# A second copy of the high parts in PSUM for the subtraction of the split products

## The chip, the cores and the metric

The kernel runs on one core of a Trainium2 chip. The metric is the device time of one execution in microseconds, taken as the median over runs. TensorE (PE) multiplies, VectorE (DVE), ScalarE (ACT) and GpSimd (POOL) do elementwise work, and SyncE (SP) issues the DMAs. SBUF is the on-chip memory, PSUM the memory of eight banks into which PE writes its products.

## The reference, cut to what is computed

One layer of a hybrid trunk on a sequence of 1024 rows of 1024 channels, float32. Four token mixers are fed by one projection, merged by gates and projected; an FFN with a short convolution follows.

```python
h = rms_norm(x, tm_pre_g) * (1.0 + sc_t) + sh_t
p = split_columns(h @ w_in)
y_ml, y_gla, y_conf, y_sc = ...        # mLSTM, gated linear attention, Conformer and short convolution
gates = jax.nn.sigmoid(p["gate"] + merge_gate_b).reshape(B, S, 4, D)
y = (gates[:, :, 0] * y_ml + ... + gates[:, :, 3] * y_sc) @ w_o
x = x + g_t * rms_norm(y, tm_post_g)
h = rms_norm(x, cm_pre_g) * (1.0 + sc_c) + sh_c
a, v = jnp.split(causal_dwconv(h @ w_up, dw_w), 2, axis=-1)     # width 3, hidden 2816
x = x + g_c * rms_norm((jax.nn.silu(a) * v) @ w_down, cm_post_g)
```

## The kernel before

Everything is held transposed, channels on the 128 partitions, and the rows of the sequence in two halves of 512. A matrix product in float32 is made of products of a reduced-width type (fp32r): each operand is split into a high part (the operand rounded, a cast on ACT) and a low part (the operand minus its high part, a subtraction on DVE or POOL), and a product of one 128-row slab is three matmuls, hi by hi, hi by lo and lo by hi. The function split (line 255) makes the two parts; wsplit, wslab, h_split, split2, tsplit and wpair call it. The high and low parts of weights lie in the tags wh and wl (four buffers each) or fh and fl (six), those of the moving operand in B11, B21, B22 and T1 to T4. The large products are computed by a 2x2 block scheme with seven products in place of eight, so that sums and differences of blocks are formed on POOL and DVE beforehand, and then split.

The stages follow one another: a first part with the conditioning and the norm (0 to 125 us), the projections and mixers P and G, the gated merge E, the output projection with the first products of the FFN O, the up-projection F (22 rounds, from the 17th on all seven products, before that five), and the down-projection W (four accumulators of 11 steps for each product; in the code p1, a second one with the same accumulators, p5, p3, p6, p7, p4). In a round of F the products with the weights s2a, s2b, s2c and s2d stand beside the evictions of the round and the width-3 convolution of the round before: ACT's first tap (an activation from SBUF into a PSUM bank), two multiply-adds on DVE on that bank, and a Silu on ACT. The last product of a round, "22" (finish, line 1536 and after), is issued in the next round, and its eviction feeds the third and fourth tap. In W the step's two operands are loaded, summed on DVE (p5, p7) or POOL (p3, p6, p4, and r2 in p5), and split; then 12 matmuls follow.

A scheduler places the instructions on the engines. Only what ordered names is kept in the program's order: POOL in P and G, PE in W. Each engine works its queue in order. All loads are on SP's queue. PSUM is one pool with eight banks, each 128x512 floats, and mps (line 180) takes the next one; ps1 and ps2 in W are four accumulators each, so the eight banks of W are held from its start.

Each operation goes through one wrapper, so that its line reads L157, and the tiles' names tell it apart (numbers of buffers left out: b is a PSUM bank, c a four-buffer work tile of the tag c4).

Of the kernel before, what the change touches and what calls it, by code (L numbers as in the profile page):

```python
# [9 lines left out]
F32 = mybir.dt.float32  # L10
F32R = mybir.dt.float32r
U32 = mybir.dt.uint32
AF = mybir.ActivationFunctionType
ALU = mybir.AluOpType
# [130 lines left out]
def trunk_layer(ctx: ExitStack, tc: tile.TileContext, I, out, dump=None, stop=None):  # L145
# [15 lines left out]
    V, A, G, T = (InOrder(e, n) for e, n in ((nc.vector, "V"), (nc.scalar, "A"), (nc.gpsimd, "G"), (nc.tensor, "T")))  # L161
# [7 lines left out]
    def new(tag, shape, dt=F32, bufs=1, pool=sb):  # L169
        uid[0] += 1  # L170
        return pool.tile(shape, dt, tag=tag, name=f"{tag}_{uid[0]}", bufs=bufs)

    c4 = lambda shape=(P, S): new("c4", list(shape), bufs=4)
    def pool(name):
        st = ctx.enter_context(ExitStack())
        return st, st.enter_context(tc.tile_pool(name=name, bufs=1))
# [3 lines left out]
    mps = lambda: new("b", [P, HS], bufs=8, pool=pb_)  # L180
# [26 lines left out]
    def pc(nm, n=0, w=1):  # L207
        o = PCOL[nm][0] + n
        return par[:, o:o + w]
# [41 lines left out]
        nc.sync.dma_start(dst, d.partition_broadcast(P))  # L251

    vl, hl, pe_last = [None], [None], [None]

    def split(src, hi, lo, eng=None, bias=None):
        if bias is None:
            hl[0] = A.copy(hi, src).ins
            vl[0] = (eng or V).tensor_tensor(lo, src, hi.bitcast(F32), ALU.subtract).ins
        else:
            A.activation(hi, src, AF.Identity, bias=bias)  # L260
            last[0] = V.scalar_tensor_tensor(lo, src, bias, hi.bitcast(F32), ALU.add, ALU.subtract).ins

    def wsplit(src, eng=None):
        hi = new("wh", [P, HS], F32R, bufs=4)
        lo = new("wl", [P, HS], F32R, bufs=4)
        split(src, hi, lo, eng)
        return hi, lo
# [20 lines left out]
    def h_split(nm, kk, src, eng=None, bias=None):  # L288
        split(src, *BM[nm][kk], eng, bias)
# [115 lines left out]
    def scaled(k):  # L405
        sc = mod[:, 8 + k:9 + k]
        x1 = xt[:, k, HH[1]]
        hi0 = A.activation(X(k, 0)[0], xt[:, k, HH[0]], AF.Copy, scale=sc).ins
        if k == 0:
            with tc.issue_after(hi0):  # L410
                square(0)
        A.activation(x1, x1, AF.Copy, scale=sc)
        split(x1, *X(k, 1), G)
        if k == 0:
            for i in (1, 2):
                with tc.issue_after(hi0):
                    std_slab(i, 0)
            more(0)
# [110 lines left out]
    def operands():  # L529
        t2 = [t[:, i, :] for t in (c4((P, 2, HS)), c4((P, 2, HS))) for i in range(2)]  # L530
        for kk in range(4):
            normed(kk, 1, G)
            with tc.issue_after(los[4 + kk]):
                normed(kk + 4, 1)
            G.tensor_tensor(xh(kk, 0), xh(kk, 1), xh(kk, 0), ALU.subtract)
            G.tensor_tensor(t2[kk], xh(kk + 4, 1), xh(kk, 0), ALU.subtract)
            yield
        new_bm("T2")
        for kk in range(4):
            h_split("T2", kk, t2[kk], bias=bias(kk + 4))  # L540
            if kk % 2:
                yield
        new_bm("T1")
        for kk in range(4):
            h_split("T1", kk, xh(kk, 0), G)
            G.tensor_tensor(xh(kk, 1), xh(kk + 4, 1), xh(kk, 1), ALU.subtract)
            V.tensor_tensor(xh(kk + 4, 0), t2[kk], xh(kk + 4, 0), ALU.subtract)
            if kk % 2:
                yield
        new_bm("T3")  # L550
        for kk in range(4):
            h_split("T3", kk, xh(kk, 1), bias=shd[:, kk:kk + 1])
            if kk % 2:
                yield
        new_bm("T4")
        for kk in range(4):
            h_split("T4", kk, xh(kk + 4, 0), G)
        new_bm("22")
        for kk in range(4):
            h_split("22", kk, xh(kk + 4, 1), bias=bias(kk + 4))  # L560
        yield
# [90 lines left out]
    mgp.close()  # L652

    ordered[0] = IN_ORDER["P"]

    mxp, mx = pool("mxp")
    s1 = lambda shape=(P, MIX): new("s1", list(shape), bufs=5, pool=mx)
# [698 lines left out]
    exp_.close()  # L1356

    ordered[0] = IN_ORDER["O"]

    fzp, fz = pool("fz")  # L1360
    dx1 = new("dx1", [P, KT, S], pool=dr)
# [145 lines left out]
    ffp, ff = pool("ff")  # L1507

    ordered[0] = IN_ORDER["F"]
    def conv_pair(n, ca, cv):  # L1510

        t = c4()
        for src, w in ((cv, NF + n), (ca, n)):
            for h in range(2):
                o = h * HS
                p_ = mps()
                A.activation(p_, src[:, o + 2:o + 2 + HS], AF.Copy, scale=pc("fdw", 3 * w + 2))
                V.scalar_tensor_tensor(p_, src[:, o + 1:o + 1 + HS], pc("fdw", 3 * w + 1), p_, ALU.mult, ALU.add)
                V.scalar_tensor_tensor(t[:, HH[h]] if w > n else p_, src[:, o:o + HS], pc("fdw", 3 * w), p_,
                                       ALU.mult, ALU.add)  # L1520
                if w == n:
                    A.activation(p_, p_, AF.Silu)
                    V.tensor_tensor(t[:, HH[h]], p_, t[:, HH[h]], ALU.mult)
        nc.sync.dma_start(dg[n], t)
# [8 lines left out]
    for n in range(NF):  # L1533
# [37 lines left out]
        if prev:  # L1571
            conv_pair(*prev[0:3])
# [10 lines left out]
        V.scalar_tensor_tensor(cv[:, lo_], pd, -1.0, u2, ALU.mult, ALU.add)  # L1583
    finish(prev)
    conv_pair(*prev[0:3])
    if stop == "F":
        return
# [34 lines left out]
    def keep():  # L1622
        ts = [new("acc", [P, 2, HS], bufs=8, pool=dn) for _ in range(2)]
        vs = [t[:, i, :] for t in ts for i in range(2)]
        pair_of.update((id(v), ts[i // 2]) for i, v in enumerate(vs))
        return vs
# [5 lines left out]
    def split2(t, a, eng):  # L1632
        th = [new("B21", [P, HS], F32R, bufs=8) for _ in range(2)]
        split(t, *th)
        return th, wsplit(a, eng)

    def mm(ps, kk, d, th, wh, new_):
        for i, (w_, t_) in enumerate(((wh[0], th[0]), (wh[0], th[1]), (wh[1], th[0]))):
            lm[0] = T.matmul(ps[d], w_[:, d * P:(d + 1) * P], t_, start=(new_ and kk == 0 and i == 0),
                             stop=(kk >= NK - 1 - LE and i == 2), skip_group_check=not new_ or kk > NK - 1 - LE).ins  # L1640

    def run(ps, operands, new_, eng=None, each=None):
        for kk in range(NK):
            th, wh = split2(*operands(kk), eng)
            for d in range(4):
                mm(ps, kk, d, th, wh, new_)
            if each:
                each(kk)

    g11, g12, g22, r1, r2 = ([None] * NK for _ in range(5))  # L1650
    ps1, ps2 = [mps() for _ in range(4)], [mps() for _ in range(4)]

    def p1(kk):
        g11[kk], r1[kk] = load(slot(), g(kk, 0, 0)), load(slot(), w(kk, 0, 0))
# [11 lines left out]
    def p5(kk):  # L1666
# [5 lines left out]
        G.tensor_tensor(r2[kk], a22, r1[kk], ALU.subtract)  # L1672
        return g11[kk], a22

    run(ps2, p5, True)
    c22 = keep()
    for d in range(4):
# [29 lines left out]
    def p6(kk):  # L1707
        G.tensor_tensor(g11[kk], g22[kk], g11[kk], ALU.subtract)
        return g11[kk], r2[kk]

    run(ps1, p6, True)
    for d in range(4):
        V.tensor_tensor(c12[d], ps1[d], c12[d], ALU.add)
# [22 lines left out]
    def last_norm(kk):  # L1736
        if kk == LN[0]:
            fin["s"] = col_sums(ssq[:, 1, :], 4)
            fin["r"] = rstd_cols(fin["s"], 4, 1.0 / D, V)
        elif kk == LN[1]:  # L1740
            bc = mps()
            rows_bc(fin["r"], 4, bc)
            fin["b"] = sqt()
            A.copy(fin["b"], bc)
# [7 lines left out]
    def p4(kk):  # L1752
        b21, a22 = raw_t(g(kk, 1, 0)), raw_a(w(kk, 1, 1))
        G.tensor_tensor(b21, g11[kk], b21, ALU.subtract)
        return b21, a22

    ends, vls = [], []
    for kk in range(NK):
        th, wh = split2(*p4(kk), None)
        vls.append(vl[0])  # L1760
        if kk < NK - LE:
            for d in range(4):
                mm(ps2, kk, d, th, wh, True)
        else:
            ends.append((kk, th, wh))
        last_norm(kk)
# [96 lines left out]
```

## Time and profile before

| | us |
|---|---|
| median of 3 runs (1699.42 to 1703.8) | 1703.27 |
| the profiled execution | 1701.04 |
| its span | 1698.9 |
| PE busy in the span | 1565.2 |
| DVE busy | 1372.5 |
| POOL busy | 878.5 |
| ACT busy | 709.6 |

The mean clock granted to PE was 0.954 of its full 2.4 GHz. The span is the time between the first and the last instruction of the trace; 2.1 us lie around it. Durations in a timeline include the pipeline of an instruction, so that two in a row overlap by some 0.08 us: their distance is the time that the engine gives to one.

### The profile page before, as it was taken

To read this page: it belongs to the slowest core of one execution; us is meant where nothing else is said; L and a number is where in the kernel's file an instruction comes from. 1 tells how busy PE (TensorE), PEld (TensorE's weight loads), DVE (VectorE), ACT (ScalarE), POOL (GpSimd) and SP (SyncE) were. 2 spreads that over 40 slices of the span, in tenths; PEclk is the share of its full clock that TensorE was granted. 3 is DMA by queue.
4 is the path that set the end of the run, shared out by engine and by line. 5 is a ranking of instruction groups with operands and counts; after the bars stand their busy time and mean duration, and the time that the engine had idled before them with its cause. 6 is when DMAs were issued, how large, how long until landed. Compare 5 with 4: busy or idle time off the path is not lost.

```text
span 1698.9 us, 20747 instructions
## 1 busy us (share of the span) xinstructions
PE 1565.2 (92%) x6791; PEld 1248.8 (74%) x6791; DVE 1372.5 (81%) x1973; ACT 709.6 (42%) x1199; POOL 878.5 (52%) x656
## 2 busy tenths in 40 slices
PE   7689899797999999989999888999999999899996
PEld 4567687685878787778788676788777888677775
DVE  7997896898776767877785869699999777799587
ACT  6454431232544232323354444354445444344442
POOL 4656465541654445767544516456445532887134
PEclk9799999899899999999999988999999999999997
DMA  9144334423446645454524555554444327455152
GB/s 363 43 133 145 116 99 126 111 96 93 123 157 228 200 126 160 134 175 128 145 84 139 194 190 188 192 164 153 137 142 153 102 75 276 141 147 149 56 151 104
DMA packets 135743, 247.90 MB, mean 146 GB/s; under 512 B 14212, under 2 KB 33268, under 8 KB 135636
## 3 DMA queue, kind: packets, MB, share of 16 engines
q1 hardware_dynamic: 135284, 246.36, 45.8%
q8 instruction: 53, 0.87, 0.2%
q14 instruction: 54, 0.44, 0.1%
q10 hardware_dynamic: 352, 0.23, 0.1%
HBM read 196.94 MB, written 49.59 MB: 145 GB/s over the span
## 4 chain that ended last, share of the span: by engine, by line
PE 49%; DVE 25%; DMA 11%; issue 8%; ACT 3%; POOL 3%; SPq 1%; DVEq 0%; POOLq 0%; ACTq 0%
PE b L157 49%; DVE c L157 6%; DVE wl L157 3%; DVE b L157 3%; DVE B L157 3%; DVE fl L157 2%; DVE mg L157 2%; DMA s2d<-in_ada_b_dram 1%; DMA T<-dg 1%; DVE acc L157 1%; DVE T L157 1%; DMA s2b<-in_ada_b_dram 1%; ACT b L157 1%; DMA fr<-in_wu_dram 1%; DVE s2b L157 1%
## 5 line engine op out<-in xcount | busy, mean ns | idle before, releaser
L157 PE MATMUL b<-B,wh 128*128 128x512 f32 (+1 forms) x1704 | 553.4, 407 | 39.7 <-ACT B L157 15.2
L157 PE MATMUL b<-T,wh 128*128 128x512 f32 x1512 | 488.5, 403 | 10.7 <-DVE c L157 7.8
L157 PEld LDWEIGHTS b<-B,wh 128*128 128x128 f32 x1704 | 333.7, 199 | 120.6 <-ACT B L157 18.7
L157 PE MATMUL b<-B,wl 128*128 128x512 f32 (+1 forms) x840 | 342.2, 409 | 31.8 <-DVE wl L157 23.4
L157 PEld LDWEIGHTS b<-T,wh 128*128 128x128 f32 x1512 | 287.9, 192 | 81.5 <-issue 10.2
L157 PE MATMUL b<-T,wl 128*128 128x512 f32 x752 | 300.7, 401 | 8.1 <-DVE wl L157 6.8
L157 PEld LDWEIGHTS b<-B,wl 128*128 128x128 f32 x840 | 166.5, 198 | 77.3 <-DVE wl L157 31.8
L157 PEld LDWEIGHTS b<-T,wl 128*128 128x128 f32 x752 | 143.9, 191 | 45.4 <-DVE wl L157 10.7
L157 ACT CAST wh<-wr 128x512 fp32r<-128x512 f32 x159 | 97.2, 617 | 148.9 <-PE b L157 107.8
L157 DVE TENSOR_TENSOR wl<-wr,wh 128x512 fp32r<-128x512 f32 x129 | 116.1, 903 | 36.8 <-ACT wh L157 36.5
L157 PE MATMUL b<-T,fh 128*128 128x512 f32 x368 | 115.7, 396 | 0.2 <-ACT fh L157 0.2
L157 POOL TENSOR_TENSOR mg<-mg,c 128x512 f32<-128x512 f32 x48 | 72.9, 1546 | 75.4 <-DVE c L157 74.1
L157 DVE SCALAR_TENSOR_TENSOR b<-c,par,b 128x512 f32<-128x512 f32 x132 | 96.6, 748 | 12.9 <-ACT b L157 12.7
L157 DVE TENSOR_TENSOR c<-b,c 128x512 f32<-128x512 f32 x128 | 87.0, 682 | 12.0 <-PE b L157 9.4
L157 DVE SCALAR_TENSOR_TENSOR b<-G,par,b 128x512 f32<-128x512 f32 x120 | 89.6, 747 | 1.3
L157 PE MATMUL b<-B,wbh 128*128 128x512 f32 x256 | 81.1, 404 | 4.2 <-ACT wbh L157 4.2
L157 PEld LDWEIGHTS b<-T,fh 128*128 128x128 f32 x368 | 68.9, 188 | 17.4 <-ACT fh L157 0.9
L157 ACT ACTIVATE c<-c,hpar 128x1024 f32<-128x1024 f32 (+1 forms) x34 | 37.5, 1102 | 104.5 <-DVE c L157 99.4
L157 ACT ACTIVATE b<-c,par 128x512 f32<-128x512 f32 x88 | 57.6, 684 | 46.6 <-DVE c L157 45.7
L157 ACT CAST wh<-B 128x512 fp32r<-128x512 f32 x66 | 40.6, 618 | 80.1 <-PE b L157 70.4
L157 PE MATMUL b<-T,fl 128*128 128x512 f32 x184 | 72.3, 396 | 0.0
L157 PE MATMUL b<-B,fh 128*128 128x512 f32 x208 | 65.7, 397 | 0.2 <-DVE c L157 0.2
(398 smaller groups left out, 2911.6 us busy)
## 6 DMA issues: line engine op xcount, KB each, us to landing
wr<-in_wu_dram SPq DMA_DIRECT2D x70, 256.0 KB, 2.7
B<-in_wg_dram SPq DMA_DIRECT2D x61, 256.0 KB, 3.3
fr<-in_wu_dram SPq DMA_DIRECT2D x50, 256.0 KB, 2.7
dg<-c SPq DMA_DIRECT2D x22, 512.0 KB, 3.3
T<-in_ada_a_dram SPq DMA_DIRECT2D x16, 512.0 KB, 9.7
wr<-in_wo_dram SPq DMA_DIRECT2D x32, 256.0 KB, 2.7
wr<-in_wp_dram SPq DMA_DIRECT2D x30, 256.0 KB, 2.8
wx<-in_wp_dram SPq DMA_DIRECT2D x24, 256.0 KB, 3.2
```

The source lines that it names most:

```text
L157: ins = f(*a, **k)
```

## The change

A flag, twin, is added. While it is on, a split without bias whose subtraction goes to DVE first takes a PSUM bank h_ and has ACT copy the operand into it as fp32r; ACT then makes the high part in SBUF as before, and DVE subtracts h_ instead of the high part. The subtraction's other operand and its result stay in SBUF. Splits on POOL and splits with a bias stay as they were. The flag goes on with P, off with O and on again with F. In W the accumulators are no longer taken all at the start: four are taken for the first products, four more before p5, four before p6 and four before p4, so that four banks are left for twins. 374 casts into PSUM are added to ACT's queue (1176 instructions become 1550); DVE's and PE's numbers are about what they were.

```diff
+    twin = [False]
     def split(src, hi, lo, eng=None, bias=None):
         if bias is None:
+            h_ = hi.bitcast(F32)
+            if twin[0] and eng in (None, V):
+                h_ = mps()
+                A.copy(h_.bitcast(F32R), src)
             hl[0] = A.copy(hi, src).ins
-            vl[0] = (eng or V).tensor_tensor(lo, src, hi.bitcast(F32), ALU.subtract).ins
+            vl[0] = (eng or V).tensor_tensor(lo, src, h_, ALU.subtract).ins
...
     ordered[0] = IN_ORDER["P"]
+    twin[0] = True
...
     ordered[0] = IN_ORDER["O"]
+    twin[0] = False
...
     ordered[0] = IN_ORDER["F"]
+    twin[0] = True
...
-    ps1, ps2 = [mps() for _ in range(4)], [mps() for _ in range(4)]
+    four = lambda: [mps() for _ in range(4)]
+    ps1 = four()
...
+    ps2 = four()
     run(ps2, p5, True)
...
+    ps1 = four()
     run(ps1, p6, True)
...
+    ps2 = four()
     for kk in range(NK):
         th, wh = split2(*p4(kk), None)
```

The scheduler places the new casts. On ACT in a round of F, before (the three activations into b are taps, the ones from b to b the Silu, the casts to wh and fh the high parts):

```order
L157 ACTIVATE b_10051<-c_2026_9938,par_74 128x512
L157 ACTIVATE b_10055<-c_2026_9938,par_74 128x512
L157 ACTIVATE b_10059<-c_2025_9937,par_74 128x512
L157 CAST wh_10107<-s2b_10102 128x512
L157 CAST wh_10111<-s2a_10101 128x512
L157 CAST wh_10116<-s2c_10103 128x512
L157 CAST wh_10120<-fr_10099 128x512
L157 CAST fh_10127<-s2d_10104 128x512
L157 ACTIVATE b_10059<-b_10059 128x512
L157 ACTIVATE b_10065<-c_2025_9937,par_74 128x512
```

and in the same part of a round now (the casts to b are the twins):

```order
L157 ACTIVATE b_10864<-c_2314_10734,par_74 128x512
L157 CAST fh_10912<-s2b_10907 128x512
L157 CAST fh_10918<-s2a_10906 128x512
L157 CAST fh_10925<-s2c_10908 128x512
L157 CAST fh_10931<-fr_10904 128x512
L157 ACTIVATE b_10864<-b_10864 128x512
L157 CAST fh_10938<-s2d_10909 128x512
L157 ACTIVATE b_10870<-c_2314_10734,par_74 128x512
L157 CAST b_10914<-s2b_10907 128x512
L157 CAST b_10920<-s2a_10906 128x512
L157 CAST b_10927<-s2c_10908 128x512
L157 CAST b_10940<-s2d_10909 128x512
```

The high parts stand where they stood; the four twins, and with them what DVE subtracts, stand behind the fourth tap.

On ACT between the last rounds of F and the first steps of W, before (B to the left of an arrow from B is the high part of W's moving operand):

```order
L157 ACTIVATE b_11871<-c_2412_11712,par_74 128x512
L157 ACTIVATE b_11865<-b_11865 128x512
L157 CAST B_2462_11947<-B_2461_11944 128x512
L157 CAST B_2466_11969<-B_2461_11944 128x512
L157 ACTIVATE b_11871<-b_11871 128x512
L157 CAST B_2470_11991<-B_2461_11944 128x512
L157 CAST wh_11995<-B_2461_11944 128x512
L157 CAST B_2474_12013<-B_2461_11944 128x512
L157 COPY c_2446_11878<-b_11731 128x512
L157 ACTIVATE b_11911<-c_2447_11879,par_74 128x512
```

and now:

```order
L157 ACTIVATE b_12395<-c_2689_12363,par_74 128x512
L157 ACTIVATE b_12399<-c_2689_12363,par_74 128x512
L157 ACTIVATE b_12403<-c_2688_12362,par_74 128x512
L157 CAST wh_12505<-B_2699_12424 128x512
L157 ACTIVATE b_12409<-c_2688_12362,par_74 128x512
L157 CAST b_12429<-B_2699_12424 128x512
L157 CAST B_2705_12451<-B_2699_12424 128x512
L157 ACTIVATE b_12403<-b_12403 128x512
L157 CAST b_12453<-B_2699_12424 128x512
L157 CAST b_12477<-B_2699_12424 128x512
L157 ACTIVATE b_12409<-b_12409 128x512
```

Before, the first casts of W stood ahead of the four taps of the last convolution (the last row is its first tap); now the first twin, b_12429, stands behind the fourth of these taps (c_2688 and c_2689 are now what c_2446 and c_2447 were).

## Rows read from the trace of the kernel before

**Rows 1.** The page's first part: busy us, share of the span, instructions.
```profile
PE 1565.2 (92%) x6791; PEld 1248.8 (74%) x6791; DVE 1372.5 (81%) x1973; ACT 709.6 (42%) x1199; POOL 878.5 (52%) x656
```

**Rows 2.** The page's chain of work that ended last, shares by engine.
```profile
PE 49%; DVE 25%; DMA 11%; issue 8%; ACT 3%; POOL 3%; SPq 1%; DVEq 0%; POOLq 0%; ACTq 0%
```

**Rows 3.** Busy time of PE, PEld, DVE, ACT, POOL in P, E, F, W.
```profile
125.00:520.00 395.00, 361.58 (x1708) 290.66 (x1707) 320.71 (x550) 147.22 (x246) 197.23 (x162) 0.95 0.39 119
520.00:945.00 425.00, 409.25 (x1747) 329.20 (x1746) 315.16 (x478) 155.37 (x243) 235.14 (x158) 0.97 0.51 154
...
1100.00:1437.00 337.00, 335.16 (x1435) 268.81 (x1435) 292.67 (x420) 156.40 (x267) 158.52 (x155) 1.00 0.45 145
1437.00:1699.00 262.00, 230.33 (x1003) 186.81 (x1001) 211.04 (x236) 110.78 (x202) 146.54 (x90) 0.93 0.42 131
```

**Rows 4.** PE's waits in W: us in total, times, longest.
```profile
PE b L157 <- POOL wl L157: 5.9, 3, 2.0
PE b L157 <- DVE wl L157: 4.0, 4, 1.3
...
PE b L157 <- DVE B L157: 2.8, 3, 1.2
```

**Rows 5.** Timeline of POOL and DVE, end of F and W: start, us, operation.
```profile
1433.51 1.29 POOL L157 TENSOR_TENSOR wl<-B,wh 128x512 fp32r<-128x512 f32 x1 [6.84 <-ACT wh L157]
...
1541.94 1.77 DVE L157 TENSOR_TENSOR wl<-s2d,wh 128x512 fp32r<-128x512 f32 x1
1543.64 1.75 DVE L157 TENSOR_TENSOR B<-T,B 128x512 fp32r<-128x512 f32 x1
...
1543.13 1.71 POOL L157 TENSOR_TENSOR s2b<-s2b,c 128x512 f32<-128x512 f32 x1
```

**Rows 6.** Timeline of ACT and PE at the wait for acc in W.
```profile
1544.87 0.62 ACT L157 CAST wh<-s2b 128x512 fp32r<-128x512 f32 x1 [2.23 <-POOL s2b L157]
1545.39 1.55 ACT L157 COPY acc<-b 128x512 f32<-128x512 f32 x3
...
1546.03 0.80 PE L157 MATMUL b<-B,wh 128*128 128x512 f32 x2 [3.09 <-ACT acc L157]
```

**Rows 7.** DVE by shape: whole run, W (2), E, F, P; busy us, mean ns.
```profile
L157 DVE TENSOR_TENSOR c<-b,c 128x512 f32<-128x512 f32 x128 | 87.0, 682 | 12.0 <-PE b L157 9.4
...
L157 DVE TENSOR_TENSOR B<-T,B 128x512 fp32r<-128x512 f32 x32 | 37.6, 1174 | 12.7 <-ACT B L157 12.7
...
L157 DVE TENSOR_TENSOR wl<-T,wh 128x512 fp32r<-128x512 f32 x7 | 4.8, 687 | 0.0
...
L157 DVE TENSOR_TENSOR wl<-B,wh 128x512 fp32r<-128x512 f32 x46 | 45.3, 984 | 0.4 <-ACT wh L157 0.4
...
L157 DVE TENSOR_TENSOR fl<-s2d,fh 128x512 fp32r<-128x512 f32 x18 | 18.5, 1029 | 1.5 <-ACT fh L157 1.5
...
L157 DVE TENSOR_TENSOR wl<-wr,wh 128x512 fp32r<-128x512 f32 x33 | 30.0, 910 | 13.4 <-ACT wh L157 13.4
```

**Rows 8.** ACT by shape, whole run: busy us, mean ns, idle before.
```profile
L157 ACT CAST wh<-wr 128x512 fp32r<-128x512 f32 x159 | 97.2, 617 | 148.9 <-PE b L157 107.8 <-POOL wr L157 19.2 <-DMA wr<-in_wg_dram 11.7
L157 ACT ACTIVATE b<-c,par 128x512 f32<-128x512 f32 x88 | 57.6, 684 | 46.6 <-DVE c L157 45.7 <-DMA c<-dsv 0.8
...
L157 ACT ACTIVATE b<-b 128x512 f32<-128x512 f32 x44 | 25.5, 580 | 59.5 <-DVE b L157 59.5
```

**Rows 9.** Busy time of the engines in three stretches of W, columns as above.
```profile
1452.00:1468.00 16.00, 10.05 (x36) 7.13 (x34) 15.90 (x10) 3.27 (x6) 16.00 (x11) 0.89 0.01 4
...
1508.00:1550.00 42.00, 34.09 (x115) 25.12 (x114) 41.35 (x31) 15.39 (x27) 37.16 (x23) 0.84 0.41 119
...
1550.00:1600.00 50.00, 50.00 (x222) 41.38 (x221) 31.66 (x43) 24.65 (x44) 10.10 (x6) 1.00 0.33 99
```

**Rows 10.** PE's waits in E: us in total, times, longest.
```profile
PE b L157 <- DVE c L157: 6.1, 3, 2.1
PE b L157 <- DVE wl L157: 5.3, 3, 2.6
```

## The prediction

> **What bounds the kernel now.** I read the page's busy shares first, then the chain, then busy time by stage, what TensorE (PE) waits for in each stage, and last the timeline where it waits most. PE is busy 92% of the span [rows 1], and half of the chain is its matmuls; VectorE (DVE) is a quarter, ScalarE (ACT) 3% [rows 2]. So the most that DVE's relief can give is PE's idle time and the slow matmuls that follow a gap. By stage PE is idle 395.0−361.6 = 33.4 us in P (projections), 425−409.3 = 15.8 in E, 337−335.2 = 1.8 in F (up-projection rounds) and 262−230.3 = 31.7 in W (down-projection) [rows 3]. F is bound by PE though DVE is 87% busy there; W is where something other than PE ends last. Its named waits are lo parts from POOL and from DVE [rows 4].
>
> The timeline of W shows why. With both inputs in SBUF a DVE subtraction takes 1.75 to 1.77 us while POOL runs an operation of its own, which then takes 1.71; POOL alone takes 1.29 [rows 5]. The same subtraction takes 0.69 where it is undisturbed (x7 in W), and an operation with one input in PSUM takes 0.68 on the mean over 128 of them, which lie in stages where POOL is 47 to 55% busy [rows 3, 7]. So the two engines serialise on pairs of SBUF operands: in 1.7 us each finishes one operation, some 1.25 of it POOL's and 0.45 DVE's. Over the 128 subtractions of W that is 131.7 us instead of 128x0.682 = 87 (groups from B<-T x32, 1174 ns, to wl<-T x7, 687 ns [rows 7]).
>
> **What the change does, part by part.** 374 subtractions read a twin in PSUM instead of the hi tile.
>
> DVE, removed: with each subtraction at the 0.682 of the one-PSUM rows, W is relieved of 131.7−87.3 = 44 us; E of 31 (46 at 984 ns, and smaller groups at 829 and more); F of 24 (94 subtractions, the largest group 18 at 1029); P of 12 (60, the larger group 33 at 910) [rows 7]. About 110 us of DVE busy time go. Bounds: 0.68 holds (−110), or the subtraction stays as slow as now (0). I take −110, by the 128 rows. The trace has no row in which PSUM costs DVE more: 0.682 with PSUM against 0.687 without [rows 7]. The Trainium skill speaks against this (Perfetto Trace Analysis, section Optimizing Scalar/DVE Operations): it gives DVE some 125 ns of overhead per instruction on PSUM against 60 on SBUF, which would put 374x0.065 = 24 us back onto DVE, an estimate from that page. The rows show no such difference, so the sum goes without it; with it the gain in W would shrink by some 8 us of DVE time.
>
> ACT, added: 374 casts into PSUM. The cast into SBUF takes 617 ns, an activation from PSUM to PSUM 580 [rows 8]; no row has SBUF to PSUM, so between these: 217 to 231 us, 42% busy becomes about 55%. In W a step of the product needs four casts instead of two, 4x0.6 = 2.4 us against 12 matmuls at 50.0/222 = 0.225, 2.7 us [rows 9]: it fits, barely, and so ACT becomes the second-busiest engine there. Every cast queued ahead of an eviction or a convolution tap delays that by 0.6.
>
> The place of the twins. Eight PSUM banks are handed out in program order, so a twin cannot run a whole round ahead as the hi casts do. In F the four twins now stand on ACT right behind the fourth tap's activation (the order shows it). The lo parts of the next round's first weight are then needed 25 matmuls after the closing product of the round before, 25x335.2/1435 = 5.8 us [rows 3]; the way there is an eviction (0.68), the tap (0.68), the twin (0.62), the subtraction (0.68), with a handover of about 0.1 each (a copy of 1.55 us for three, so 0.52 each from 1545.39, frees PE at 1546.03 [rows 6]): 3.1 us [rows 7, 8]. It is covered by 2.7 us: F costs and gains **0**.
>
> From F to W the cover is two matmuls, not 25: the first lo part of W comes behind the same way, so PE stands about 3.1−0.5 = 2.6 us and then runs slowly for a while; before, the cast stood ahead. I count 4.5 with the slow matmuls. Against it: just behind, from 1452 to 1468, PE waits on POOL's lo parts, 36 matmuls in 16 us [rows 4, 9], so 16−36x0.225 = 7.9 are lost; POOL works on through a stall of PE, so what PE loses at the boundary it does not lose there. POOL's own gain is 0.45 for each DVE subtraction that stops sharing, one per step of three POOL operations, some six from 1439 on: 2.7. Net of the two between −2.7 (all absorbed) and +1.8 (none): I take **−1.5**, nearer to the absorbed end, since POOL is busy 16.0 of those 16.0 us [rows 9].
>
> 1508 to 1550: 115 matmuls in 42 us, lost 42−115x0.225 = 16.1; DVE is busy 41.35 of it, with 31 operations [rows 9]. Of these 22 are split subtractions, and 16 of them stand at 1.75 or more, like the two in the timeline [rows 5]: at 0.6 apart instead of 1.7, DVE is freed of 16x1.1 = 18 us, and POOL of 0.45 for each. PE's waits on DVE's B and wl end there. The one wait on ACT's acc copy (3.09) is the same cause: that copy stood on ACT behind a cast that waited 2.23 for POOL [rows 6]; POOL, with 23 operations almost back to back, is some 16x0.45 = 7 us earlier. What stays is the pairs of plain additions, still both in SBUF. I take three quarters: **−12**; bounds −16 and −5 (the DVE waits alone, 4.0+2.8 [rows 4], less the lengthening of ACT). Other waits on wl and B behind 1600: **−2**. Starts of the later products: the twin's bank comes from the accumulators of the product before, four copies of 0.52, then twin 0.62, subtraction 0.68 and handovers, 4.3 us, against 15 to 18 matmuls of cover (3.4 to 4.1): three starts at 0.7, **+2**.
>
> E: PE waits 5.3 us in three for wl and 6.1 in three for c [rows 10]. The subtractions for wl shorten by 0.3 on the mean, up to 1.1, with several in a row: 4 of the 5.3 go, and about 2 of the slow matmuls behind them; the branches' starts wait for a twin's bank, cover 16 to 25 matmuls: back +2. **−4**, bounds −9 and +4. P: relief of 12 on 321 busy, waits mostly for chains of evictions that the change leaves: **−2**, bounds −5 and +3.
>
> Sum: 0−1.5−12−2+2−4−2 = −19.5 us, say −18 since ACT in W has little room. Against the profiled execution of 1701.0 (span 1698.9) that is 1683; the median of before is 2.2 higher, so **1685**.
>
> **The rivals.** (a) Slower: F's cover breaks. ACT takes its queue in order, and if the way from the closing product to the lo part is over 5.8 us (a second cast or an activation ahead of the twin would do it, 2x0.65, and DVE's queue of some 20 operations per round the rest), PE stands in each of 22 rounds. The point is 2.7 us more than I count; 1 us beyond it is 22 us, less the 19: 1706; 1.5 us beyond gives 1717. Against it: ACT is only 46% busy in F [rows 3], 63% with 94 twins. For it: DVE at 87%.
> (b) No change: the plain additions of DVE (two for each step in W's third product) keep POOL as slow as it is, the waits for POOL stay, and the boundary stall is not absorbed: −5−2+2+1.8, with P and E at 0, about −3: 1700.
> (c) More: all of W's stalls but the ends' go, with the slow matmuls (−16−2.7−2 without loss at starts), E at −9 and P at −4: −33, 1670.
> (d) The change does not do what it says: DVE stays blocked by POOL with one operand in PSUM too; then ACT's casts and the starts are cost alone: 4.5+2+4 = +10, 1714. Against it stand the 128 rows at 682 with both engines busy.
>
> **How the numbers follow.** Forecast (−10 to −25) 0.46; (a) 0.13; (b) 0.20; (c) 0.15; (d) 0.06. What a measurement here can tell from no change is about 0.3%, 5 us: 1698.2 to 1708.4 counts as the same. Faster: 0.46+0.15 and the fast edge of (b), 0.05: 0.66. Same: the rest of (b) and the near part of (a): 0.19. Slower: 0.15. The range leaves out the far part of (c) and what lies beyond 1708: 1670 to 1708; of the forecast alone 1678 to 1694.
>
> **What would show it.** Right: DVE's split subtractions at 0.68 in every group; DVE busy near 1260 and ACT near 930; PE's waits for DVE wl and B in W near nothing, the clock granted in 1508 to 1550 at 1.00 instead of 0.84 [rows 9]; F still at 14 us a round with PE idle under 3. Wrong: waits of PE for fl, wl or B in each round of F; subtractions with a PSUM operand at over 0.8; ACT acc or ACT c growing among PE's waits; W longer than 258 us.

## The result and the profile after

The changed kernel takes 1672.8 us (median of 4 runs, 1669.4 to 1676.2), against 1701.4 for the kernel before in the same comparison: 0.983 of it, 95% interval 0.981 to 0.986. It is 28.5 us faster, where 18 were forecast; 1672.8 lies in the range of 1670 to 1708, near its fast end, and outside the 1678 to 1694 of the forecast alone. The profiled execution took 1670.4 us, with a span of 1668.7.

The first part of the page, which answers to [rows 1]:

```profile
span 1668.7 us, 21151 instructions
...
PE 1549.8 (93%) x6791; PEld 1237.9 (74%) x6791; DVE 1258.7 (75%) x1973; ACT 897.9 (54%) x1573; POOL 816.1 (49%) x656
```

DVE lost 1372.5−1258.7 = 114 us of busy time, near the 110 forecast. ACT gained 188 where 217 to 231 were forecast: summed over the instructions its durations grew by 218, but busy time counts what two of them in a row overlap only once. ACT's instructions rose by the 374 twins. POOL lost 62 us, though it executes the same 656 instructions. Three rows of the groups by shape: a subtraction that now reads a twin (b), a POOL operation, and a twin (columns: count, busy us, mean ns, idle before):

```profile
L157 DVE TENSOR_TENSOR B<-T,b 128x512 fp32r<-128x512 f32 x32 | 21.8, 682 | 13.3 <-PE b L157 5.9 <-ACT b L157 4.5 <-DMA c<-dg 2.4
...
L157 POOL TENSOR_TENSOR mg<-mg,c 128x512 f32<-128x512 f32 x48 | 62.8, 1329 | 74.2 <-DVE c L157 73.9
...
L157 ACT CAST b<-wr 128x512 fp32r<-128x512 f32 x73 | 42.9, 587 | 33.7 <-DVE c L157 13.9 <-POOL wr L157 6.1 <-DMA wr<-dg 5.3
```

The subtraction B<-T took 1174 ns before [rows 7] and takes 682 now; the mean of every one of the 26 groups with a twin lies between 677 and 692. POOL's mg<-mg,c, which the change does not touch, took 1546 ns on the mean before and takes 1329: beside DVE's subtractions from PSUM it is slowed less.

Busy time by stage, the columns of [rows 3], for P, E, F and W (P, E and O end at the same matmuls as before within two; the border of F and W is set where W's stall begins, 18 matmuls earlier than in [rows 3]):

```profile
125.00:510.00 385.00, 359.36 (x1717) 289.27 (x1716) 307.94 (x554) 176.92 (x305) 188.54 (x163) 0.96 0.39 122
510.00:929.00 419.00, 405.99 (x1747) 325.67 (x1746) 286.75 (x478) 199.65 (x332) 214.96 (x157) 0.98 0.50 155
...
1084.00:1420.50 336.50, 330.89 (x1419) 266.01 (x1418) 267.48 (x417) 202.19 (x358) 145.56 (x156) 1.00 0.45 147
1420.50:1669.00 248.50, 226.81 (x1019) 186.07 (x1019) 162.34 (x239) 177.72 (x335) 123.47 (x90) 0.95 0.44 138
```

W became 13.5 us shorter, E 6, P 10; F hardly. The table further down compares at equal matmuls. PE's waits in W, which answer to [rows 4]:

```profile
PE b L157 <- DVE B L157: 7.8, 2, 4.4
PE b L157 <- DVE rs L157: 3.0, 1, 3.0
PE b L157 <- DVE wl L157: 3.0, 4, 1.2
PE b L157 <- POOL wl L157: 0.9, 1, 0.9
```

POOL's lo parts hold PE up for 0.9 us instead of 5.9. DVE B, however, holds it longer than before, 7.8 us instead of 2.8. One of its two waits, of 3.4, lies in the last product, where DVE has four operations on acc in front of the subtraction, as it had before, when PE waited 1.0 and 1.3 there. The other, of 4.4, is new and lies where W begins. The timeline there, of ACT, DVE and PE (start, us, operation):

```profile
1418.54 0.69 ACT L157 ACTIVATE b<-c,par 128x512 f32<-128x512 f32 x1 [1.59 <-DVE c L157]
1419.16 0.57 ACT L157 CAST b<-B 128x512 fp32r<-128x512 f32 x1
...
1417.82 0.69 DVE L157 TENSOR_TENSOR c<-b,mi 128x512 f32<-128x512 f32 x1
...
1419.07 1.41 DVE L157 SCALAR_TENSOR_TENSOR b<-c,par,b 128x512 f32<-128x512 f32 x2
1420.39 0.68 DVE L157 TENSOR_TENSOR B<-B,b 128x512 fp32r<-128x512 f32 x1
...
1416.36 0.39 PE L157 MATMUL b<-B,wh 128*128 128x512 f32 x1
1421.13 0.80 PE L157 MATMUL b<-B,wh 128*128 128x512 f32 x1 [4.38 <-DVE B L157]
```

Here the way from the last product of F to the first lo part of W can be read off: eviction at 1417.82, the fourth tap on ACT at 1418.54, the twin at 1419.16, the subtraction at 1420.39, behind two multiply-adds that DVE had in its queue, and PE goes on at 1421.13.

To see where a kernel gains or loses, the table compares the start of the n-th matmul of PE with that of the n-th in the kernel before, both from the profiled executions (worked out from the records of PE, counted from 0; negative is earlier). The columns after "after" are the experiments below.

| n, place | before, us | after | W only | unread | P only | no F | O too | late W | p1 on DVE | late W, p1 on DVE |
|---|---|---|---|---|---|---|---|---|---|---|
| 2050, end of P | 519.1 | −10.1 | 1.2 | −1.3 | −8.2 | −6.7 | −10.2 | −7.6 | −8.6 | −11.0 |
| 3750, end of E | 933.8 | −16.1 | 3.6 | 13.5 | −6.9 | −9.8 | −12.7 | −17.5 | −15.3 | −18.4 |
| 4350, start of F | 1098.3 | −15.2 | 4.1 | 13.8 | −4.1 | −8.7 | 74.3 | −14.1 | −11.2 | −14.5 |
| 5700, end of F | 1416.2 | −16.5 | 2.6 | 14.8 | −6.5 | −11.6 | 72.5 | −15.1 | −12.2 | −15.9 |
| 5850, W begun | 1450.7 | −9.2 | 8.9 | 15.0 | −6.5 | −4.8 | 79.7 | −15.1 | −4.4 | −15.9 |
| 6000 | 1493.7 | −16.8 | 1.3 | 17.4 | −7.0 | −12.3 | 71.9 | −19.4 | −12.8 | −22.7 |
| 6300 | 1577.9 | −29.1 | −10.9 | 14.9 | −6.0 | −24.4 | 59.7 | −31.6 | −25.0 | −33.9 |
| last | 1689.6 | −30.7 | −13.8 | 21.1 | −5.5 | −27.2 | 58.0 | −32.7 | −26.4 | −33.6 |

Single executions differ by a few us in P and E: over the nine whose P has the same twins (seven of the columns, and one more execution each of the changed kernel and of the last column, described at the end of the experiments) the entry at 2050 lies between −6.2 and −11.0. From 5700 to the last, two executions of one kernel differ by 2.2 at most (−14.2 and −16.4 of the changed kernel).

### The profile page after: what moved, and what is told of

The parts are those of the page before. It is cut to its first block, busy times and chain, and to the rows that moved or that the text cites. A ratio compares the mean times of both kernels' runs of the same rounds, so it can differ in the third digit from the quotient of the medians.

```text
span 1668.7 us, 21151 instructions
## 1 busy us (share of the span) xinstructions
PE 1549.8 (93%) x6791; PEld 1237.9 (74%) x6791; DVE 1258.7 (75%) x1973; ACT 897.9 (54%) x1573; POOL 816.1 (49%) x656
## 4 chain that ended last, share of the span: by engine, by line
PE 59%; DVE 11%; DMA 7%; issue 6%; ACT 3%; POOL 2%; SPq 0%; DVEq 0%; POOLq 0%; ACTq 0%
PE b L157 59%; DVE c L157 2%; DVE wl L157 2%; DMA T<-dg 1%; DVE acc L157 1%; DVE T L157 1%; DVE b L157 1%; DVE mg L157 1%; DMA s2b<-in_ada_b_dram 1%; DMA s2b<-dnm 1%; DMA s2c<-in_ada_b_dram 1%; DVE B L157 1%; DVE s2a L157 1%; DMA wr<-in_wu_dram 1%; ACT b L157 1%
## 5 line engine op out<-in xcount | busy, mean ns | idle before, releaser
L157 PE MATMUL b<-B,wh 128*128 128x512 f32 (+1 forms) x1704 | 547.2, 404 | 36.8 <-ACT B L157 15.8
L157 PEld LDWEIGHTS b<-B,wh 128*128 128x128 f32 x1704 | 328.6, 196 | 115.6 <-ACT B L157 19.9
L157 PE MATMUL b<-B,wl 128*128 128x512 f32 (+1 forms) x840 | 337.0, 403 | 28.3 <-DVE wl L157 27.1
L157 POOL TENSOR_TENSOR mg<-mg,c 128x512 f32<-128x512 f32 x48 | 62.8, 1329 | 74.2 <-DVE c L157 73.9
L157 DVE TENSOR_TENSOR c<-b,c 128x512 f32<-128x512 f32 x128 | 87.3, 685 | 13.5 <-PE b L157 8.7
L157 DVE TENSOR_TENSOR wl<-wr,wh 128x512 fp32r<-128x512 f32 x79 | 75.7, 964 | 18.7 <-ACT wh L157 18.5
L157 POOL TENSOR_TENSOR B<-B,B 128x512 f32<-128x512 f32 x29 | 42.4, 1463 | 58.0 <-DVE wl L157 51.4
L157 ACT CAST wh<-wx 128x512 fp32r<-128x512 f32 x53 | 32.7, 618 | 62.3 <-PE b L157 44.9
```

Source lines behind the costliest of these rows:

```text
L157: ins = f(*a, **k)
```

## The experiments

**Only the casts.** Everything is made as in the change, but DVE subtracts the high part in SBUF; no one reads the twins.

```diff
-            vl[0] = (eng or V).tensor_tensor(lo, src, h_, ALU.subtract).ins
+            vl[0] = (eng or V).tensor_tensor(lo, src, hi.bitcast(F32), ALU.subtract).ins
```

> All 374 casts into PSUM are made, but DVE subtracts the high part in SBUF as before, so nothing reads the twins. Theory (the gain is DVE's relief from POOL): no gain; DVE busy back at 1370, and the price of the casts and banks alone, 0 to 15 us over the kernel before, 1700 to 1715. Rival (the gain is the new order of the queues, above all the 10 us in P, where two waits of 4.8 and 3.8 us went): P keeps its 8 to 10 us, and the whole stays at 1690 or below.

1723.7 us against 1705.0 for the kernel before beside it, 1.012 of it (1.009 to 1.015). The page:

```profile
PE 1560.1 (91%) x6790; PEld 1240.9 (72%) x6791; DVE 1364.5 (79%) x1973; ACT 898.9 (52%) x1573; POOL 865.5 (50%) x656
```

ACT is as busy as in the changed kernel, DVE nearly as in the kernel before. So the casts that nobody reads bring no gain: this kernel is 19 us slower than the one before, and 19+28.5, some 47, slower than the change. It was dearer than expected (0 to 15): the table shows −1 in P, 15 us in E and 6 in W.

The experiment does not hold the order of the queues fixed, since the scheduler placed the instructions anew. In W PE's order is the program's, and 4 of its 1090 matmuls stand otherwise than in the change (none differs between before and change); the 6.3+14.2 = 20.5 us between the two kernels there are not PE's order, though the other engines' queues differ as well. In P and E, however, 340 of 1705 and 212 of 1700 places in PE's queue hold a product of other tiles here than in the change. And the −1.3 of P is a net. The change gains most between the 1150th and the 1200th matmul (7.3 us) and between the 1800th and the 1850th (6.5); with the casts alone the same stretches gain 4.5 and 3.8, and from the 550th to the 600th 5.9 are lost, where the change loses 3.1. So the rival is not out in P.

**P alone.** Twins in P and G, none in E, F, W; the accumulators of W are still taken late.

```diff
     ordered[0] = IN_ORDER["E"]
+    twin[0] = False
...
     ordered[0] = IN_ORDER["F"]
-    twin[0] = True
+    twin[0] = False
```

> Twins in P and G alone. Theory (the 10 us that P gained are the relief of its 60 subtractions): the first 2000 matmuls are 8 to 10 us earlier than in the kernel before, 1691 to 1693 in all. Rival (P gains by where the scheduler happened to put things, which depends on the rest too): the 2000th matmul less than 4 us earlier, or more than 12.

1695.2 us, 0.994 (0.992 to 0.996), which is 9.8 less than the kernel before beside it (1705.0); the 2050th matmul comes 8.2 us earlier. The time itself is a little over the band of 1691 to 1693, and in the profiled execution E and O gave 4 back. The twins of P are enough for P's gain. From the 5700th matmul to the last it changes by 1.0: the late allocation of the accumulators alone does nothing.

**W alone.**

```diff
     ordered[0] = IN_ORDER["P"]
-    twin[0] = True
+    twin[0] = False
...
     ordered[0] = IN_ORDER["F"]
-    twin[0] = True
+    twin[0] = False
...
     ordered[0] = IN_ORDER["W"]
+    twin[0] = True
```

> Twins in W alone; P, G, E and F are as in the kernel before. Theory (W's gain is its own: DVE and POOL no longer share): the gain from the first of W's accumulator copies to the end stays, 12 to 15 us below the kernel before, so about 1687; DVE busy falls by about 45 us to 1327. Rival (the gain of W is in part the order that the twins of F leave behind, or the earlier start of DVE's queue): under 8 us. The start of W should lose less than the 7 us that the changed kernel loses there, since the last convolution of F has no twins beside it, or just as much, if the stall is that of W's own first twins.

1690.5 us, 0.992 (0.989 to 0.995), 14.6 below the kernel before beside it. From the end of F to the last matmul 2.6+13.8 = 16.4 us are won, in the changed kernel 14.2; DVE's busy time is 1317.7, 55 us less, where 45 were expected. W's gain is its own. Where W begins PE waits the same 4.4 us for DVE B and falls back 6.3 us instead of 7.3, so the stall comes from W's own first twins and not from those of F.

**Without F.** Twins in P, G, E and W.

```diff
     ordered[0] = IN_ORDER["F"]
-    twin[0] = True
+    twin[0] = False
...
     ordered[0] = IN_ORDER["W"]
+    twin[0] = True
```

> The changed kernel without the twins of F (P, G, E and W have them). Theory (F is bound by PE and gains nothing from its 94 twins; its relief of DVE by 24 us is idle time): F's length unchanged within 1.5 us, 1672 to 1676 in all. Rival (DVE at 87% in F was already costing PE something): F gets 3 us or more longer, 1677 or more.

1674.6 us, 0.982 (0.979 to 0.985), the same as the changed kernel. F takes 2.9 us less than in the kernel before without twins and 1.3 less with them (4350 to 5700). F's 94 twins bring nothing, and cost at most the 1.6 us between these two executions.

**The output projection too.**

```diff
     ordered[0] = IN_ORDER["O"]
-    twin[0] = False
+    twin[0] = True
```

> The changed kernel with twins in the output projection too. Theory (a stage gains what its waits for contended subtractions cost, and its banks are held by accumulators): O has 20 us of PE idle time in 155, mostly in the norms, so between 2 us gain and 6 us loss. Rival (PSUM's banks are no limit, DVE's relief pays as in W): 4 us or more faster.

1757.2 us, 1.033 of the kernel before (1.031 to 1.035): 84 us slower than the change, and both expectations miss it. Nearly all of it lies between the 3750th and the 4350th matmul, that is in O, in two kinds of places. PE's waits from 930 to 1170 us:

```profile
PE b L157 <- DVE wl L157: 60.8, 7, 17.6
PE b L157 <- DVE B L157: 37.1, 1, 37.1
```

In the first place PE waits 17.6 us for a first lo part, then at each of five products in a row 6.95 (7.3 from one matmul's start to the next), then 8.4. ACT and DVE at the first of the five:

```profile
947.94 0.60 ACT L157 ACTIVATE c<-b 128x512 f32<-128x512 f32 x1 [2.96 <-PE b L157]
948.43 0.68 ACT L157 ACTIVATE c<-b,mod 128x512 f32<-128x512 f32 x1
949.00 0.69 ACT L157 ACTIVATE mg<-b,mod 128x512 f32<-128x512 f32 x1
952.07 0.81 ACT L157 ACTIVATE mg<-c,mod 128x512 f32<-128x512 f32 x1 [2.38 <-DVE c L157]
952.92 0.59 ACT L157 CAST b<-mg 128x512 fp32r<-128x512 f32 x1
953.44 0.61 ACT L157 CAST B<-mg 128x512 fp32r<-128x512 f32 x1
953.96 1.10 ACT L157 CAST b<-wr 128x512 fp32r<-128x512 f32 x2
...
954.58 1.29 DVE L157 TENSOR_TENSOR wl<-wr,b 128x512 fp32r<-128x512 f32 x2 [0.35 <-ACT b L157]
```

The twin of the next weight (b<-wr) stands on ACT behind the whole chain that ends one product: its eviction, the activations with mod, DVE's c and the twin of mg. Banks are given in the program's order, so that it stands behind them, and the lo part comes only after each product. In the second place PE stands 37 us; until 1084, with 27 of them still to come, DVE works on eight operations without twins (mg<-c,mg), and then ACT and DVE make the FFN's moving operands one after the other, twins among them. Which part of the 37 is the twins' own was not separated. The first place is the mechanism of rival (a), in another stage. It shows what leaving O out saves, and that a stage with cover must be looked for, not assumed. The Trainium skill (ScalarE: Activation LUTs, section Step-by-step: what each stage is for) recommends PSUM as ACT's faster destination with the caveat that it pays only where TensorE leaves most of PSUM free. The traces agree with the first: a cast takes 577 to 592 ns on the mean of its groups into PSUM, and 613 to 624 into SBUF. O fits the caveat, as far as its banks are what delays the twins.

**The start of W without twins.** The first four steps of W subtract from SBUF.

```diff
     ordered[0] = IN_ORDER["W"]
+    twin[0] = False
...
             th, wh = split2(*operands(kk), eng)
+            if kk == 3:
+                twin[0] = True
```

> The changed kernel with the twins of the first four steps of W left out (their subtractions read the high part in SBUF). In the changed kernel PE stands 4.8 us where W begins, and is 7.3 us behind until it catches up with POOL's lo parts 150 matmuls on. Theory (the stall is that of W's first twins, and it is absorbed, since PE would wait for POOL later otherwise): the stall goes to under 1 us, POOL's stretch gets its waits back, and by the 6000th matmul nothing is won: within 2 us of the changed kernel, 1671 to 1675. Rival (the recovery behind the stall was DVE's relief, and the two are independent): 5 to 7 us faster, 1666 to 1668.

1669.2 us, 0.982 (0.981 to 0.984). The stall is gone; PE's waits from 1412 to 1470 us are now

```profile
PE b L157 <- POOL wl L157: 3.7, 3, 2.1
```

instead of 4.4 for DVE B and 0.9 for POOL. Between the 5700th and the 6000th matmul it wins 4.3 us where the changed kernel wins 0.3, so of the stall's 7.3 us 3.3 were absorbed and 4.0 were a loss (the four steps lose their own relief too, so the loss may be larger). The theory (all absorbed) and the rival (none) are both too simple: less than half was hidden. On the whole time the difference from the change is within its interval.

**W's first weights on DVE.** In the first two products of W the weights' lo parts move from POOL to DVE, with twins.

```diff
-    run(ps1, p1, True, G)
+    run(ps1, p1, True)
...
-    run(ps1, lambda kk: (raw_t(g(kk, 1, 0)), raw_a(w(kk, 0, 1))), False, G)
+    run(ps1, lambda kk: (raw_t(g(kk, 1, 0)), raw_a(w(kk, 0, 1))), False)
```

> The changed kernel with the weights of W's first two products split on DVE (with twins) instead of POOL. Theory (POOL's three operations a step bound the first 20 steps of W): POOL has two operations left, and after the stall at W's start PE waits for nothing until 1500; but that stall was absorbed by POOL's backlog and the kernel after waited for POOL only 0.9 us there, so the gain is 0 to 2 us. Rival (DVE with its plain additions becomes the bound, since it has four operations a step): 2 to 5 us slower.

1673.8 us, 0.985 (0.983 to 0.986), as the change; from 5700 to 6000 it wins 0.6. With the stall in place, POOL is no longer what ends last there.

**Both.** No twins in the first four steps, and from the fifth on the weights on DVE.

```diff
-            th, wh = split2(*operands(kk), eng)
+            th, wh = split2(*operands(kk), eng if not twin[0] else None)
+            if kk == 3:
+                twin[0] = True
```

> Both edits: no twins in the first four steps of W, and from the fifth step on the weights of W's first two products on DVE with twins. Theory (stall and POOL's backlog are two bounds on the same stretch, so that only taking both away pays): 4 to 7 us faster than the changed kernel, 1666 to 1669, where each edit alone gives under 2. Rival (DVE's queue is the third bound): under 2 us here too.

1667.9 us, 0.982 (0.980 to 0.983). It wins 6.8 us between 5700 and 6000, against 0.3, 4.3 and 0.6 for the change and the two edits alone; that each edit alone would give under 2 did not hold for the first. Some 3 us are given back from 6000 on; 1 us of it is at two waits for wl, where PE's starts lie 2.2 and 1.9 us apart instead of 1.4 and 1.6. Since P and E differ by more than that between executions, both were run again side by side, five rounds:

> The changed kernel once more, beside the next run on the same chip: 0.981 to 0.986 of the kernel before.

> No twins in the first four steps of W, and from the fifth on the weights of W's first two products on DVE with twins, once more. If the 6 us that its trace gains between the 5700th and the 6000th matmul are real, its median is 4 to 7 us below that of the changed kernel beside it; if what differs between single traces in P and E covers it, under 2 us.

The changed kernel 1674.6 (0.981 to 0.985 of before), this one 1673.2 (0.980 to 0.984). The stretch from 5700 to 6000 repeats, 6.1 against 1.4, but the whole differs by 1.4 us with intervals that overlap. A stretch of W is shown to be shorter; a faster kernel is not.

## Why the prediction was right, and where its sizes were off

**The mechanism.** The premise was that two SBUF operands make DVE and POOL take turns and that one PSUM operand ends it. All 26 groups at 677 to 692 ns, with POOL at 49% busy, bear it out, and with them rival (d) is out. In W, where PE's order is the same in the kernel before and in the change, the relief is what the experiments leave as the cause: W's twins alone win 16.4 us there, and the same casts unread lose 6.3. No overhead of PSUM on DVE appears: 682 with a twin, against 687 for the undisturbed wl<-T before [rows 7], so the 24 us that the prediction estimated from the Trainium skill (Perfetto Trace Analysis, section Optimizing Scalar/DVE Operations) are not there.

**The range, and some luck.** By the traces the last matmul starts 30.7 us earlier: P (with what lies before it) −10.1, E −6.0, O +0.9, F −1.3, W −14.2, where −2, −4, 0, 0 and −13.5 were forecast. That is more than the forecast's own bound of −25 and near rival (c), −33; but (c) had W at −20.7 and P at −4, and W came as forecast. The time lies in the range because (c) had widened it, and P, which neither counted so high, took it there: this is luck. Rivals (a) and (b) fall with F's −1.3 and W's −14.2.

**W.** Forecast −1.5, −12, −2 and +2, together −13.5; measured −14.2 (16.5 to 30.7). The stretch from the 6000th to the 6300th matmul, with the starts, was to give −10 and gave −12.3; the tail −2, gave −1.6. The changed kernel in the stretch that answers to the one at 0.84 [rows 9]:

```profile
1491.00:1526.00 35.00, 32.35 (x139) 25.83 (x140) 23.76 (x35) 30.52 (x58) 29.95 (x23) 1.00 0.57 166
```

DVE is busy 23.8 of 35 us instead of 41.4 of 42, and the clock granted is 1.00 instead of 0.84. Before, ten distances of over 0.47 us between matmul starts lost 10 of the 16.1 us, and the slower matmuls among the rest the other 6; now 2.9 us are lost in all, of them under 1 outside such distances. The wait for acc fell from 3.09 to 0.4. ACT is busy 30.5 of 35 us here, so it fits, barely. One sign of being right did not come: PE's waits for DVE wl and B in W were to be near nothing, and are 3.0 and 7.8 us, because of the boundary and of the last product.

**The boundary.** 4.5 counted with the slow matmuls, 7.3 measured. The way was taken as 3.1 us; it is 4.77 from the last matmul's start to the next. Missing were 1.46 between that start and the eviction's, in which DVE worked off two multiply-adds, and the 0.6 by which its queue held the subtraction; the steps themselves took 2.7 instead of 3.1. The stall was to be hidden behind POOL's backlog; the net, −1.5 forecast and −0.3 and −1.4 measured (two executions, 5700 to 6000), came out near, but the experiment on the start of W shows that only 3.3 of 7.3 were hidden. Two errors offset, which is luck again: a longer stall, and a relief of POOL that without the stall gave 4.3 and not the 2.7 counted.

**F.** 0 forecast; −1.3 with twins, −2.9 without. Right, but with less cover than counted. A round of F in the changed kernel, PE and DVE (start, us, operation):

```profile
1206.64 0.39 PE L157 MATMUL b<-B,fl 128*128 128x512 f32 x1
...
1212.95 0.39 PE L157 MATMUL b<-T,wl 128*128 128x512 f32 x1
...
1210.49 0.68 DVE L157 TENSOR_TENSOR wl<-s2b,b 128x512 fp32r<-128x512 f32 x1
```

The closing product's last matmul starts at 1206.64, the first lo part is made by 1211.17, and PE takes it at 1212.95: the way is 4.5 us instead of the 3.1 counted, and 1.8 are left instead of 2.7. The twin is ready at 1209.00; the subtraction stands behind an eviction in DVE's queue. In the first place of O there was no such cover.

**P: the term that was mis-sized.** E was −4 and gave −6.0 here, −1.6 to −9.9 over the executions with these twins, so −4 lies in the spread. P was −2, with a bound of −5, and gave −10.1 (−6.2 to −11.0). P's step that failed is "waits mostly for chains of evictions that the change leaves". PE's waits in P after the change:

```profile
PE b L157 <- DVE s L157: 6.2, 3, 2.1
PE b L157 <- POOL mi L157: 5.2, 1, 5.2
PE b L157 <- ACT c L157: 4.4, 1, 4.4
PE b L157 <- ACT G L157: 3.4, 1, 3.4
PE b L157 <- DVE s2b L157: 3.2, 3, 1.7
PE b L157 <- DVE c L157: 2.3, 2, 1.4
PE b L157 <- DMA p<-dgv: 0.7, 1, 0.7
PE b L157 <- POOL wl L157: 0.2, 1, 0.2
```

and before, of the two that matter:

```profile
PE b L157 <- DVE c L157: 9.5, 4, 4.4
PE b L157 <- ACT c L157: 5.7, 3, 3.4
```

The waits for evictions by DVE (c) fell from 9.5 us to 2.3. The two stretches that gain most, 7.3 and 6.5 us, are those of the 4.4 for DVE c and of the 3.4 for ACT c; both waits are gone. (The 4.4 for ACT c that is left is another, of 1.7 before, and costs 3.1.) This is the first of the two places in the kernel before, on DVE and POOL:

```profile
319.26 0.76 DVE L157 SCALAR_TENSOR_TENSOR b<-G,par,b 128x512 f32<-128x512 f32 x1
322.24 1.51 DVE L157 TENSOR_TENSOR s2b<-s2b,cols 128x512 f32<-128x512 f32 x1 [2.22 <-POOL s2b L157]
323.67 0.41 DVE L157 TENSOR_TENSOR V<-b,dn 128x256 f32<-128x256 f32 x1
324.01 0.74 DVE L157 SCALAR_TENSOR_TENSOR b<-G,par,b 128x512 f32<-128x512 f32 x1
324.66 0.68 DVE L157 TENSOR_TENSOR c<-b,c 128x512 f32<-128x512 f32 x1
...
320.94 1.26 POOL L157 TENSOR_TENSOR s2b<-s2b,cst 128x512 f32<-128x512 f32 x1 [6.96 <-PE b L157]
```

DVE stood idle 2.2 us for POOL while PE waited for an eviction further back in DVE's queue. But POOL's operation was not slowed by DVE: it took 1.26 us, and POOL had stood idle for 7 us before it, until a product of PE was there. In the changed kernel PE's products stand in another order around this place, as in 346 of the 1705 places of P. So what the prediction took for fixed, the chains of evictions, is what gave way. That the twins of P are enough, and that unread casts are not, the experiments show. Whether the relief of DVE and POOL (13 and 9 us of busy time in P) gives the gain, or the order that the scheduler makes with the twins, is not separated and stays open; a run of the old kernel in the new order would tell.

In E the same is open: PE's order differs there too, in 276 of 1700 places from the kernel before. Nor is it settled why the casts alone cost E 15 us; there PE waits 13.4 us for DVE c instead of 6.1, 4.4 for ACT b instead of nothing, and 1.5 more for DVE wl.

## What to carry to other kernels

Where two engines take turns on operand pairs in one memory, moving one operand elsewhere relieved both here: count the busy time of the one that is not edited, too. A copy that needs a scarce buffer, handed out in program order, could not be made ahead, so follow its whole queue, stage by stage, from the product that frees the bank to the matmul that wants the result, with everything that stands before it on the way, and leave out stages where that way is longer than the work that covers it. A bound that hides a stall should be tested by removing the stall: part of it may be a loss. And where a scheduler places the instructions, an experiment that takes one thing away may also change the order; compare the order before calling the rest the cause.

## What the runs showed of the hardware

A cast from SBUF takes ACT 577 to 592 ns into PSUM and 613 to 624 into SBUF, by the means of the groups. A DVE subtraction of 128x512 with one operand in PSUM took 677 to 692 ns on the mean in all 26 groups, with POOL busy for 49% of the span, where the 32 of the group B<-T with both in SBUF, in the kernel before, took 678 to 1787. A POOL operation beside such a pair took 1.71 us, and one alone 1.29 [rows 5]; with the twins mg<-mg,c fell from 1546 to 1329 ns on the mean, T<-B,T from 1724 to 1434. Not expected was the price of the way that a bank takes: 4.8 us from the start of a last matmul to the start of the one that needs a lo part made from the bank, and 7.3 us for each product where ACT's chain of activations stands between.
